# Two gate blocks in four by seven products, the retention norm on POOL and ScalarE, and gates that end with their chunks

## The chip, the core and the metric

One Trainium2 chip, one NeuronCore of it. TensorE (PE) multiplies, VectorE (DVE), ScalarE (ACT) and GpSimd (POOL) do the elementwise work, SyncE (SP) issues most of the transfers. Matrix products are accumulated in PSUM, eight banks of 128 x 512 float32. The metric is the device time of one execution in microseconds; lower is better. The kernel before takes 2174.5 us, the median of three runs (2174.4 to 2176.41).

## What is computed

A decoder block on 1024 tokens of width 1024 in float32: normalization and modulation, two token mixers side by side (chunkwise retention and dilated window attention), a gated merge, and an MLP. The change touches the retention mixer, four heads with key width 256 and value width 512, in chunks of 128 tokens:

```python
def step(state, inp):
    qi, ki, vi = inp
    s = jnp.einsum('bhid,bhjd->bhij', qi, ki) * inner_decay[None]
    o = (jnp.einsum('bhij,bhje->bhie', s, vi)
         + jnp.einsum('bhid,bhde->bhie', qi, state) * q_decay[None, :, :, None])
    state = (state * chunk_decay[None, :, None, None]
             + jnp.einsum('bhjd,bhje->bhde', ki * k_decay[None, :, :, None], vi))
    return state, o
...
ro = retention(rq, rk, heads(rv, RET_HEADS))
mu = jnp.mean(ro, axis=-1, keepdims=True)
var = jnp.mean(jnp.square(ro - mu), axis=-1, keepdims=True)
ro = ((ro - mu) * lax.rsqrt(var + GN_EPS)).transpose(0, 2, 1, 3).reshape(B, S, RET_V_W)
ro = (ro * gn_g.astype(jnp.float32) + gn_b.astype(jnp.float32)).astype(h.dtype)
ret_out = (jax.nn.silu(rg) * ro) @ w_ret_out
```

`rg` is a projection of the same normalized input to 2048 columns: 16 gate blocks of 128 columns, four for each head.

## The kernel before

Every float32 product is made of three products of rounded halves: a number is split into a high part (a copy on ACT) and a low part (a subtraction on DVE), and low x high, high x low and high x high are summed in PSUM (`mm3`, L207, L209, L211). One such product has 128 x 128 weights and 512 columns.

The stages follow one another, each written out in the order in which its engines are to work; every engine runs its own instructions in that order and waits where its inputs or a buffer are not ready. First values, then `queries_keys`, then `values`, then 32 steps `chunk(h, c)` (head h, chunk c), then attention, merge and MLP.

`queries_keys` runs a list of pairs (`PAIRS`). A pair is two blocks of 128 output columns against all 1024 inputs and tokens, done by a scheme that replaces eight block products by seven (`Blocks`, the seven in `ORDER`): 7 x 4 x 3 = 84 products in place of 2 x 48 = 96, for some additions and subtractions of weights and results on DVE. Queries, keys, attention queries, most branch gates and one Silu gate block of each head (`s_pairs`, two pairs) are made so and written to DRAM. After each product of a pair from item 116 on, and after each group of twelve products in `values`, `mod_turn` may issue an adaLN weight load on SP and reduce the one before on DVE.

A chunk (`chunk`) issues, on TensorE: the two halves of the new key-value product (`kv`), gate steps, scores and key transposes of the next chunk (`s_kt`), the output (`o`, from the carried state and from the scores), the four transposes of the chunk before's normalized output (`on_T`), and a last gate step. A gate step (`rg_mm`) is one of the eight k-slices of a gate block, six products; three blocks of each head are made in the chunks, 24 steps a head (`RG`), and a block's weights are split a step ahead by `ahead`. On the other engines: the state update on DVE (L743, L745) and its split on ACT and DVE (L749, L750); the split of the weights (L197, L198); the scores' decay and split and the keys' (L652 to L668); the queries' split on ACT and POOL (L616, L617); the statistics of the output and its normalization (L772 to L778), with POOL's power in between. In the first four chunks of a head, `u_final` finishes a quarter of the head before: two affine passes on ACT (L688), the multiplication with the Silu gate on DVE (L690), a store (L691).

PSUM in this stage: two double banks for gate blocks, and four single ones for everything else in a chunk, handed out as they come free. SBUF: a ring of twelve buffers of 128 x 1024 (`etile`) for transposed outputs and Silu gates.

Of the kernel before, what the change touches and what calls it, by code (L numbers as in the profile page):

```python
# [17 lines left out]
P = 128  # L18
# [22 lines left out]
CS_QD = 132  # L41
CS_QD2 = 136
# [98 lines left out]
def block_kernel(ctx, tc, io, stop=None, dbg=None):  # L141
# [12 lines left out]
    def banks(single):  # L154
# [7 lines left out]
        PS["n"] = 8 if single else 4  # L162
# [3 lines left out]
    def ps_mm(name):  # L166
        return PS["p"].tile([P, 2, 512], F32, tag="mm", bufs=2, name=name)

# [343 lines left out]
    def etile(name, dt=F32):  # L512
        return R["p"].tile([P, 1024], dt, tag="E", bufs=12, name=name)
# [116 lines left out]
    def s_kt(i):  # L630
# [34 lines left out]
        if pk is not None:  # L665
            nc.vector.scalar_tensor_tensor(flat(kl), flat(pk), kd, fv(flat(kh)), op0=ALU.mult, op1=ALU.subtract)
            hd["k", g] = (kh, kl)
        nc.vector.tensor_sub(sml, sm, fv(smh))  # L668

    def on_T(h, c):  # L670
# [3 lines left out]
        if c == 0:  # L674
            hd["on", h] = [etile(f"on{h}{e}") for e in range(4)]
        for e in range(4):
            nc.tensor.transpose(po[:, e, :], on[:, e * P:(e + 1) * P], ident)
        for e in range(4):
            nc.scalar.copy(hd["on", h][e][:, c * C:(c + 1) * C], po[:, e, :])

    def u_final(h, es=range(4), queue=nc.sync):
        for e in es:
# [7 lines left out]
            nc.vector.tensor_mul(t, t, hd["srg", h, e])  # L690
            queue.dma_start(y_d[h][:, 2 * (i % 2):2 * (i % 2) + 2, e // 2], t.rearrange("p (t x) -> p t x", t=2))  # L691

    RG = ((6, 2, 2, 3, 3, 3, 3, 2),) + ((3,) * NC,) * (H - 1)

    def rg_mm(n):

        for _ in range(n):
            if hd.get("rgk", NK) == NK:
                hd["rgk"], hd["rgw"], hd["rgp"] = 0, hd["rgws"].pop(0), ps_mm("rg")
            proj_mm(hd["rgp"], hd["rgw"], [hd["rgk"]])  # L700
            hd["rgk"] += 1
            if hd["rgk"] == NK:
                hd["rgs"] = hd["rgp"]

    def rg_out(h, c):

        if "rgs" in hd:
            e = {1: 0, 2: 0, 4: 1, 5: 1, 7: 2}[c]
            hd["srg", h, e] = etile(f"srg{h}{e}")
            nc.scalar.activation(hd["srg", h, e], flat(hd.pop("rgs")), AF.Silu)  # L710
        if c == 6:
            hd["srg", h, 3] = etile(f"srg{h}3")
            nc.sync.dma_start(hd["srg", h, 3], srg_d[h])

    def chunk(h, c, ahead, w=None):
# [21 lines left out]
        rg_mm(1 if g == 0 else RG[h][c] - 1)  # L737
# [9 lines left out]
        if g > 0:  # L747
            for i in range(len(kvs)):
                nc.scalar.copy(sh1[:, i, :], st[:, i, :])  # L749
                nc.vector.tensor_sub(sl1[:, i, :], st[:, i, :], fv(sh1[:, i, :]))  # L750
        if g == 0:
            jit_qk(2)
        ahead(2)
        if 0 < g < NG - 1:
            s_kt(g + 1)
# [12 lines left out]
        rg_mm(0 if g == 0 else 1)  # L768
        bn = p.tile([P, 6], F32, tag="bn", bufs=2, name=f"bn{h}{c}")
        ba = p.tile([P, 2], F32, tag="ba", bufs=2, name=f"ba{h}{c}")  # L770
        gr = p.tile([P, 1], F32, tag="gr", bufs=2, name=f"gr{h}{c}")
# [2145 lines left out]
```

## Time and profile before

| what | value |
|---|---|
| runs | 2174.4, 2174.5, 2176.41 us |
| profiled execution, its own time | 2173.28 us |
| its span, first to last instruction | 2171.3 us |
| pairs | about 180 to 598 us |
| values | about 598 to 712 us |
| retention chunks | about 712 to 980 us |
| bytes moved by transfers | 425.18 MB, 196 GB/s in the mean |
| granted TensorE clock | 0.999 |

Read such a profile by stages. A busy share says how much an engine worked, not whether it was waited for; a gap on TensorE in one stage has its own cause, which the lists of waits name. A matrix product is shown with its whole duration, from its first to its last column through the array, while the next one starts before it ends: the rate is seen in the distance of the starts.

### The profile page before, as it was taken

Reading aid. Unit: us, or ns where it says so; the run is one execution under the profiler, and the core shown is the slowest. Engines: PE = TensorE matmul, PEld = TensorE weight load, DVE = VectorE, ACT = ScalarE, POOL = GpSimd, SP = SyncE. Lnnn points to the kernel's source line nnn. Section 1 sums busy time; section 2 is a strip of 40 time slices with the busy share of each in tenths; the row PEclk is TensorE's granted clock in tenths of the full one; section 3 lists DMA queues with packets and bytes.
Section 4 is the critical chain, followed back from the end, with each engine's and each line's share of the span. In section 5 each row is a group of like instructions: output and inputs, shape, how many; then the busy total and the mean of one; then the engine's idle time right before and its main releaser. Section 6 shows DMA issues by size and latency. Waiting matters only on the chain. (4 is left out here: it accounts for less than half of the span.)

```text
span 2171.3 us, 27289 instructions
## 1 busy us (share of the span) xinstructions
PE 2144.7 (99%) x10036; PEld 1782.4 (82%) x10036; DVE 1520.4 (70%) x2358; ACT 959.3 (44%) x1757; POOL 165.7 (8%) x199
## 2 busy tenths in 40 slices
PE   8999999999999999999999999999999999999998
PEld 6888888888887788888888888888778888888887
DVE  6886777777656677776667644677876665877855
ACT  5543322323334455556656625434454455533413
POOL 0001111100001112211110000001000000000003
PEclk9999999999999999999999999999999999999999
DMA  9859998835588744436877366653144435645322
GB/s 383 282 208 309 285 306 265 243 117 194 186 301 303 234 148 151 160 127 197 218 194 196 115 245 211 217 191 132 64 175 160 150 136 193 253 135 173 109 88 78
DMA packets 162674, 425.18 MB, mean 196 GB/s; under 512 B 28005, under 2 KB 55916, under 8 KB 159468
## 3 DMA queue, kind: packets, MB, share of 16 engines
q1 hardware_dynamic: 150264, 374.90, 48.3%
q0 software_dynamic: 9584, 48.24, 9.9%
q8 instruction: 79, 1.29, 0.2%
q10 hardware_dynamic: 2692, 0.30, 0.1%
q14 instruction: 55, 0.45, 0.1%
HBM read 324.13 MB, written 160.32 MB: 223 GB/s over the span
## 5 line engine op out<-in xcount | busy, mean ns | idle before, releaser
L207 PE MATMUL qap<-hh,qaw 128*128 128x512 f32 x264 | 102.7, 389 | 0.0
L209 PE MATMUL qap<-hl,qaw 128*128 128x512 f32 x264 | 102.7, 389 | 0.0
L211 PE MATMUL qap<-hh,qaw 128*128 128x512 f32 x264 | 102.7, 389 | 0.0
L617 POOL TENSOR_TENSOR j<-qk,j 128x512 fp32r<-128x512 f32 x32 | 42.8, 1338 | 454.8 <-ACT j L616 454.8
L2235 POOL TENSOR_TENSOR accnf<-accnf,sqnf 128x256 f32<-128x256 f32 (+1 forms) x18 | 16.6, 922 | 609.6 <-ACT sqnf L2231 609.6
L2339 ACT ACTIVATE a<-a 128x512 f32<-128x512 f32 x48 | 30.3, 631 | 72.8 <-DVE a L2338 71.3
L749 ACT CAST stateh<-state 128x512 fp32r<-128x512 f32 x54 | 32.9, 622 | 57.8 <-DVE state L745 55.7
L209 PEld LDWEIGHTS qap<-hl,qaw 128*128 128x128 f32 x264 | 49.5, 188 | 10.4
L211 PEld LDWEIGHTS qap<-hh,qaw 128*128 128x128 f32 x264 | 49.6, 188 | 10.3
L207 PEld LDWEIGHTS qap<-hh,qaw 128*128 128x128 f32 x264 | 49.5, 188 | 10.2
L2547 ACT CAST w2h<-w2s 128x512 fp32r<-128x512 f32 x36 | 22.4, 621 | 80.3 <-DVE w2s L2585 80.3
L264 DVE TENSOR_TENSOR fw<-w1r,fw 128x512 fp32r<-128x512 f32 x48 | 32.9, 688 | 33.6 <-ACT fw L254 33.6
L264 DVE TENSOR_TENSOR qaw<-wa,qaw 128x512 fp32r<-128x512 f32 x66 | 44.0, 687 | 9.4 <-ACT qaw L254 9.4
L2070 DVE TENSOR_TENSOR rwl<-rwl,rwh 128x1024 fp32r<-128x1024 f32 x25 | 30.2, 1221 | 29.0 <-ACT rwh L2100 29.0
L207 PE MATMUL fp<-h2h,fw 128*128 128x512 f32 x128 | 50.0, 390 | 0.0
L209 PE MATMUL fp<-h2l,fw 128*128 128x512 f32 x128 | 49.8, 389 | 0.0
L211 PE MATMUL fp<-h2h,fw 128*128 128x512 f32 x128 | 49.8, 389 | 0.0
L207 PE MATMUL roa<-rh,rwl 128*128 128x512 f32 x128 | 49.8, 389 | 0.0
L209 PE MATMUL roa<-rl,rwh 128*128 128x512 f32 x128 | 49.8, 389 | 0.0
L211 PE MATMUL roa<-rh,rwh 128*128 128x512 f32 x128 | 49.8, 389 | 0.0
L1603 ACT ACTIVATE P<-P,ng 128x128 f32<-128x128 f32 (+1 forms) x96 | 41.9, 438 | 17.6 <-DVE ng L1595 17.5
L292 DVE TENSOR_TENSOR qat<-qat,qap 128x512 f32<-128x512 f32 x22 | 15.1, 688 | 42.8 <-PE qap L211 35.8
(3089 smaller groups left out, 7187.8 us busy)
## 6 DMA issues: line engine op xcount, KB each, us to landing
cossin<-in_w_ada_dram SPq DMA_DIRECT2D x32, 512.0 KB, 3.5
v<-vd SPq DMA_DIRECT2D x32, 512.0 KB, 4.3
w1r<-in_w_ff_dram SPq DMA_DIRECT2D x32, 512.0 KB, 4.6
yt<-y POOLq DMA_DIRECT2D x24, 512.0 KB, 7.5
xsd<-as SPq DMA_DIRECT2D x24, 512.0 KB, 3.1
w2r<-in_w_ff2s_dram SPq DMA_DIRECT2D x24, 512.0 KB, 6.4
em<-in_w_ada_dram SPq DMA_DIRECT2D x16, 512.0 KB, 10.2
wrvs<-in_w_rv_dram POOLq DMA_DIRECT2D x16, 512.0 KB, 9.8
```

The source lines that it names most:

```text
L207: nc.tensor.matmul(o, wl, xh, start=first, stop=False, skip_group_check=skip)
L209: nc.tensor.matmul(o, wh, xl, start=False, stop=False, skip_group_check=skip)
L211: nc.tensor.matmul(o, wh, xh, start=False, stop=last, skip_group_check=skip)
L264: nc.vector.tensor_sub(t[:, 512:], src, fv(t[:, :512]))
L292: nc.vector.tensor_sub(u, u, b)
L617: nc.gpsimd.tensor_sub(t[:, 1], src, fv(t[:, 0]))
L749: nc.scalar.copy(sh1[:, i, :], st[:, i, :])
L1603: nc.scalar.activation(v, v, AF.Exp, bias=ng[:, blk:blk + 1], accum_out=st[:, g, blk, 2 + a:3 + a])
L2070: nc.vector.tensor_sub(lo, fv(lo), fv(hi))
L2235: (nc.vector if f == 7 else nc.gpsimd).tensor_add(G["acc", key], G["acc", key], sq)
L2339: nc.scalar.activation(o, o, AF.Relu)
L2547: nc.scalar.copy(hi, src)
```

## The change

Two gate blocks of each head instead of one go through the pairs (four more blocks, two more pairs; each head now loads two from DRAM, in chunks 4 and 6), so that the chunks make two blocks, 16 steps a head, spread by `RG` so that a block ends with the last step of a chunk; the Silu follows at once. In PSUM a gate block takes two of three single banks, and five serve the rest; attention opens its own layout again. The ring for Silu gates has four buffers; transposed outputs have their own four, twice as wide, and are copied by two instead of four instructions.

The normalization is rewritten as scale x o + bias on ACT. The variance gets an epsilon that holds the decay, so no decay factor is left; POOL computes minus the mean, the power, and their product. Statistics now come on DVE before the second half of the state's low part, before the weights' split (`ahead`) and before the multiplication with the Silu gate, which is put off to the next chunk; the first half of the state's low part moves into the score chain (`mid`). `mod_turn` takes a step every second turn.

```diff
-    def banks(single):
+    def banks(single, ret=False):
 
         if PS:
             PS["ctx"].close()
@@ -159,12 +159,15 @@
         PS["ctx"] = ExitStack()
         PS["p"] = PS["ctx"].enter_context(tc.tile_pool(name=f"psum{PS['i']}", bufs=2, space=bass.MemoryType.PSUM,
                                                        reuse_waits="tile"))
-        PS["n"] = 8 if single else 4
+        PS["n"] = 8 if single else 5 if ret else 4
...
+    def ps_rg(name):
+        return PS["p"].tile([P, 512], F32, tag="rg", bufs=3, name=name)
...
-        return R["p"].tile([P, 1024], dt, tag="E", bufs=12, name=name)
+        return R["p"].tile([P, 1024], dt, tag="E", bufs=4, name=name)
...
-    def s_kt(i):
+    def s_kt(i, mid=None):
...
+        if mid:
+            mid()
         nc.vector.tensor_sub(sml, sm, fv(smh))
...
         if c == 0:
-            hd["on", h] = [etile(f"on{h}{e}") for e in range(4)]
+            hd["on2", h] = [R["p"].tile([P, 2, 1024], F32, tag="EO", bufs=4, name=f"on{h}{e}") for e in range(2)]
+            hd["on", h] = [hd["on2", h][e // 2][:, e % 2] for e in range(4)]
         for e in range(4):
             nc.tensor.transpose(po[:, e, :], on[:, e * P:(e + 1) * P], ident)
-        for e in range(4):
-            nc.scalar.copy(hd["on", h][e][:, c * C:(c + 1) * C], po[:, e, :])
-
-    def u_final(h, es=range(4), queue=nc.sync):
+        for e in range(2):
+            nc.scalar.copy(hd["on2", h][e][:, :, c * C:(c + 1) * C], po[:, 2 * e:2 * e + 2, :])
+
+    def u_final(h, es=range(4), queue=nc.sync, late=False):
         for e in es:
             i = h * 4 + e
             t = hd["on", h][e]
@@ -687,30 +693,36 @@
                 b = t[:, 512 * hf:512 * hf + 512]
                 nc.scalar.activation(b, b, AF.Identity, scale=gnv[0][:, neg + i:neg + i + 1],
                                      bias=gnv[1][:, neg + i:neg + i + 1])
-            nc.vector.tensor_mul(t, t, hd["srg", h, e])
-            queue.dma_start(y_d[h][:, 2 * (i % 2):2 * (i % 2) + 2, e // 2], t.rearrange("p (t x) -> p t x", t=2))
-
-    RG = ((6, 2, 2, 3, 3, 3, 3, 2),) + ((3,) * NC,) * (H - 1)
+
+            def mul(t=t, i=i, e=e):
+                nc.vector.tensor_mul(t, t, hd["srg", h, e])
+                queue.dma_start(y_d[h][:, 2 * (i % 2):2 * (i % 2) + 2, e // 2], t.rearrange("p (t x) -> p t x", t=2))
+
+            if late:
+                return mul
+            mul()
+
+    RG = (6, 2, 2, 2, 1, 1, 2, 3), (3, 2, 2, 2, 1, 1, 2, 3), (3, 2, 2, 2, 1, 1, 2, 3), (3, 2, 2, 2, 1, 1, 1, 1)
 
     def rg_mm(n):
 
         for _ in range(n):
             if hd.get("rgk", NK) == NK:
-                hd["rgk"], hd["rgw"], hd["rgp"] = 0, hd["rgws"].pop(0), ps_mm("rg")
+                hd["rgk"], hd["rgw"], hd["rgp"] = 0, hd["rgws"].pop(0), [ps_rg(f"rg{i}") for i in range(2)]
             proj_mm(hd["rgp"], hd["rgw"], [hd["rgk"]])
             hd["rgk"] += 1
             if hd["rgk"] == NK:
-                hd["rgs"] = hd["rgp"]
+                i = hd["rgi"] = hd.get("rgi", -1) + 1
+                t = hd["srg", i // 2, i % 2] = etile(f"srg{i // 2}{i % 2}")
+                for j, ps in enumerate(hd["rgp"]):
+                    nc.scalar.activation(t[:, 512 * j:512 * j + 512], ps, AF.Silu)
 
     def rg_out(h, c):
 
-        if "rgs" in hd:
-            e = {1: 0, 2: 0, 4: 1, 5: 1, 7: 2}[c]
+        if c in (4, 6):
+            e = c // 2
             hd["srg", h, e] = etile(f"srg{h}{e}")
-            nc.scalar.activation(hd["srg", h, e], flat(hd.pop("rgs")), AF.Silu)
-        if c == 6:
-            hd["srg", h, 3] = etile(f"srg{h}3")
-            nc.sync.dma_start(hd["srg", h, 3], srg_d[h])
+            nc.sync.dma_start(hd["srg", h, e], srg_d[h, e - 2])
 
...
-        rg_mm(1 if g == 0 else RG[h][c] - 1)
+        rg_mm(1 if g == 0 else RG[h][c] - (g < NG - 1))
         for i, kv in enumerate(kvs):
             if g == 0:
                 nc.scalar.copy(sh1[:, i, :], kv)
@@ -744,15 +756,17 @@
             else:
                 nc.vector.scalar_tensor_tensor(st[:, i, :], st[:, i, :], float(GAMMA[h] ** C), kv,
                                                op0=ALU.mult, op1=ALU.add)
-        if g > 0:
-            for i in range(len(kvs)):
+        def low(i):
+            nc.vector.tensor_sub(sl1[:, i, :], st[:, i, :], fv(sh1[:, i, :]))
+
+        if g > 0 and kvs:
+            for i in range(2):
                 nc.scalar.copy(sh1[:, i, :], st[:, i, :])
-                nc.vector.tensor_sub(sl1[:, i, :], st[:, i, :], fv(sh1[:, i, :]))
         if g == 0:
             jit_qk(2)
-        ahead(2)
+            ahead(2)
         if 0 < g < NG - 1:
-            s_kt(g + 1)
+            s_kt(g + 1, (lambda: low(0)) if kvs else None)
         po = ps_s(f"o{h}{c}")
         if c > 0:
             t = hd["j", g]
@@ -765,21 +779,28 @@
             jit_qk(g + 2)
         if g > 0:
             on_T(*divmod(g - 1, NC))
-        rg_mm(0 if g == 0 else 1)
+        rg_mm(1 if 0 < g < NG - 1 else 0)
         bn = p.tile([P, 6], F32, tag="bn", bufs=2, name=f"bn{h}{c}")
         ba = p.tile([P, 2], F32, tag="ba", bufs=2, name=f"ba{h}{c}")
-        gr = p.tile([P, 1], F32, tag="gr", bufs=2, name=f"gr{h}{c}")
+        gr = p.tile([P, 3], F32, tag="gr", bufs=2, name=f"gr{h}{c}")
         nc.vector.bn_stats(bn, po)
         nc.vector.bn_aggr(ba, bn)
-        nc.vector.tensor_scalar(gr, ba[:, 1:2], ct[:, CS_QD2 + h:CS_QD2 + h + 1], GN_EPS, op0=ALU.mult, op1=ALU.add)
-        nc.gpsimd.tensor_tensor(gr, gr, mhalf[:, 0:1], op=ALU.pow)
-        nc.vector.tensor_mul(gr, gr, ct[:, CS_QD + h:CS_QD + h + 1])
+        nc.vector.tensor_scalar_add(gr[:, 0:1], ba[:, 1:2], ct[:, CS_EQ + h:CS_EQ + h + 1])
+        nc.gpsimd.tensor_tensor(gr[:, 2:3], ba[:, 0:1], ct[:, CS_NEG:CS_NEG + 1], op=ALU.mult)
+        nc.gpsimd.tensor_tensor(gr[:, 1:2], gr[:, 0:1], mhalf[:, 0:1], op=ALU.pow)
+        nc.gpsimd.tensor_tensor(gr[:, 2:3], gr[:, 1:2], gr[:, 2:3], op=ALU.mult)
+        if g > 0:
+            if kvs:
+                low(1)
+            ahead(2)
+        if "um" in hd:
+            hd.pop("um")()
+        if h > 0 and c < 4:
+            hd["um"] = u_final(h - 1, (c,), late=True)
         on = p.tile([P, DV], F32, tag="on", bufs=1, name=f"onm{h}{c}")
-        nc.vector.tensor_scalar(on, po, ba[:, 0:1], gr, op0=ALU.subtract, op1=ALU.mult)
+        nc.scalar.activation(on, po, AF.Identity, scale=gr[:, 1:2], bias=gr[:, 2:3])
         hd["o", h, c] = on
         rg_out(h, c)
-        if h > 0 and c < 4:
-            u_final(h - 1, (c,))
 
...
-    srg_d = [dram.tile([P, S], F32, name=f"srgd{h}") for h in range(H)]
+    srg_d = {(h, i): dram.tile([P, S], F32, name=f"srgd{h}{i}") for h in range(H) for i in range(2)}
...
-    s_pairs = [("s", i) for i in range(H // 2)]
+    s_pairs = [("s", i) for i in range(H)]
     PAIRS = [{"r": r_pairs, "a": a_pairs, "g": g_pairs, "k": k_pairs, "s": s_pairs}[i].pop(0)
-             for i in "rargrarkrargrarkgagass"]
+             for i in "rargrarkrargrarkgagassss"]
...
             elif pair[0] == "s":
-                dst = srg_d[2 * pair[1] + i]
+                dst = srg_d[pair[1], i]
...
-        while turn["i"] < NV + 2 and 7 * turn["n"] > 16 * turn["i"]:
+        while turn["i"] < NV + 2 and turn["n"] > 2 * turn["i"]:
...
-        banks(False)
+        banks(False, True)
...
+    RGW, n = [], 0
+    for g in range(NG):
+        RGW += [g - (g > 2)] * (n < 8 * len(RGW) + 1 <= n + RG[g // NC][g % NC])
+        n += RG[g // NC][g % NC]
     for h in range(H):
         for c in range(NC):
             steps.add((lambda h, c: lambda ahead, *w: chunk(h, c, ahead, *w))(h, c),
-                      ([wsplit(io["w_rg"][3 * h + (0, 2, 5).index(c)])] if c in (0, 2, 5) else []),
+                      ([wsplit(io["w_rg"][RGW.index(NC * h + c)])] if NC * h + c in RGW else []),
                       manual=True)
...
+            if pair == a == 0:
+                banks(False)
...
-        cst[:, CS_QD + h] = np.exp(lg * (i + 1))
-        cst[:, CS_QD2 + h] = np.exp(2 * lg * (i + 1))
+        cst[:, CS_NEG] = -1.0
+        cst[:, CS_EQ + h] = GN_EPS * np.exp(-2 * lg * (i + 1))
...
-        "w_rg": _cols(w[:, 4096:6144].reshape(1024, 4, 4, P)[:, :, :3].reshape(1024, 1536)),
-        "w_rg2": _pairs(w[:, 4096:6144].reshape(1024, 4, 4, P)[:, :, 3].reshape(1024, 512)),
+        "w_rg": _cols(w[:, 4096:6144].reshape(1024, 4, 4, P)[:, :, :2].reshape(1024, 1024)),
+        "w_rg2": _pairs(w[:, 4096:6144].reshape(1024, 4, 4, P)[:, :, 2:].reshape(1024, 1024)),
```

4 lines of the change are left out of this document (2 added, 2 removed).

## The prediction

> **What bounds the kernel now.** I read the page first, then the busy times by stage, then the waits.
>
> ```profile
> span 2171.3 us, 27289 instructions
> ...
> PE 2144.7 (99%) x10036; PEld 1782.4 (82%) x10036; DVE 1520.4 (70%) x2358; ACT 959.3 (44%) x1757; POOL 165.7 (8%) x199
> ```
>
> ```profile
> 180.00:596.00 416.00, 416.00 (x1837) 344.47 (x1836) 303.74 (x472) 122.67 (x214) 36.33 (x50) 1.00 0.74 233
> 596.00:712.00 116.00, 112.84 (x493) 91.73 (x491) 71.34 (x99) 48.01 (x71) 8.33 (x10) 1.00 0.84 308
> ...
> 783.00:850.00 67.00, 66.94 (x334) 55.83 (x333) 51.25 (x108) 36.83 (x92) 14.40 (x16) 1.00 0.48 161
> ```
>
> Columns: stretch, length, busy time of PE, weight loads, DVE, ACT, POOL, granted clock, DMA share, GB/s. TensorE has no gap in the stage of pairs (180 to 596) and none in a head of retention chunks (783 to 850); only the value stage between them (596 to 712) shows 3.2 us of gap. So TensorE sets the time, by its number of products. In the pair stage 1837 products take 416.00 us, 0.2265 us each (one lasts longer, but they overlap). In a head DVE is busy 51 of 67 us, ACT 37: covered, as long as TensorE has filler between the steps of a chunk. The filler is the gate products, and the change takes a third of it away. One chunk of head 1, TensorE's timeline:
>
> ```profile
> 806.62 0.39 PE L207 MATMUL kv<-v,kl 128*128 128x512 f32 x1
> ...
> 810.71 0.28 PE L638 MATMUL sT<-j 128*128 128x256 f32 x1
> ...
> 811.27 0.48 PE L207 MATMUL o<-stateh,j 128*128 128x512 f32 x1
> ...
> 813.44 0.60 PE L677 MATMUL oT<-ct,onm 128*128 128x128 f32 x4
> ...
> 815.27 0.39 PE L207 MATMUL kv<-v,kl 128*128 128x512 f32 x1
> ```
>
> From kv to sT 4.09 us (kv's six products 1.37, two gate steps of six 2.72), scores and key transposes 0.56, output 2.17, output transposes and the last gate step 1.83; together 8.65. With n gate steps instead of three a chunk is 8.65 - 1.36 x (3 - n): 7.29 for two, 5.93 for one.
>
> **The change part by part.**
>
> *Products.* Four gate blocks leave the chunks (4 x 48 = 192 products) and come back as two pairs of 84 (168): 24 fewer, 24 x 0.2265 = -5.4 us. The pairs' adds lie under TensorE as those of the 22 pairs there do (DVE 304 of 416 us, no gap). The Trainium skill (TensorE: Matmul & The Clock Gate, Back-to-back issue gap) has streams of weight load and product of 512 columns come down to about 131 ns each, which would make this an estimate of -3.1, and it gives 216 ns only for a product by itself. The row's 226.5 ns, in a stage without a gap, decides.
>
> *Value stage.* The adaLN loads get a step every second turn instead of every 2.29. Before, the last step falls in turn 76 of 78; after, in turn 67 of 92, a turn being 12 products or 2.72 us: 68 us before the stage ends.
>
> ```profile
> SPq L1254 <- DVE cossin L1252: 36.7, 12, 9.0
> ```
> ```profile
> PE vc L209 <- DVE vwl L1328: 1.9, 2, 1.5
> ```
>
> SP's queue stood 36.7 us around this stage behind these loads, with the value weights behind it; TensorE waited 1.9 us for such weights about 20 turns into the value stage. After, that is turn 72, past the last step. Bounds 0 and -3.1 (all the stage's gap); I take -1.0, half the wait.
>
> *Work per chunk.*
>
> ```profile
> L750 DVE TENSOR_TENSOR statel<-state,stateh 128x512 fp32r<-128x512 f32 x28 | 18.1, 689 | 1.3
> L745 DVE SCALAR_TENSOR_TENSOR state<-state,kv 128x512 f32<-128x512 f32 x24 | 15.3, 680 | 0.0
> L778 DVE TENSOR_SCALAR onm<-o,ba,gr 128x512 f32<-128x512 f32 x17 | 13.8, 810 | 1.8
> L772 DVE BATCH_NORM_STATS2 bn<-o 128x6 f32<-128x512 f32 x16 | 11.1, 695 | 3.6 <-PE o L211 3.6
> L690 DVE TENSOR_TENSOR on<-on,srg 128x1024 f32<-128x1024 f32 x8 | 9.7, 1218 | 0.1
> L666 DVE SCALAR_TENSOR_TENSOR kl<-kT,ct,kh 128x256 fp32r<-128x256 f32 x14 | 6.7, 478 | 0.0
> L668 DVE TENSOR_TENSOR sml<-sm,smh 128x128 fp32r<-128x128 f32 x16 | 4.7, 293 | 0.7 <-ACT smh L664 0.7
> L654 DVE TENSOR_TENSOR sm<-sm,decay 128x128 f32<-128x128 f32 x16 | 4.7, 292 | 0.5
> L653 DVE TENSOR_TENSOR sm<-sm,sT 128x128 f32<-128x128 f32 x16 | 4.5, 284 | 7.0 <-ACT sm L652 7.0
> ...
> L774 DVE TENSOR_SCALAR gr<-ba,ct 128x1 f32<-128x1 f32 x16 | 3.4, 214 | 0.6
> L773 DVE BATCH_NORM_AGGREGATE ba<-bn 128x2 f32<-128x6 f32 x16 | 2.9, 183 | 0.5
> L776 DVE TENSOR_TENSOR gr<-gr,ct 128x1 f32<-128x1 f32 x16 | 2.6, 160 | 14.4 <-POOL gr L775 14.4
> ...
> L198 DVE TENSOR_TENSOR raw_6675l<-raw,raw_6675h 128x1024 fp32r<-128x1024 f32 x1 | 1.2, 1227 | 0.3 <-ACT raw_6675h L197 0.3
> ```
> ```profile
> L749 ACT CAST stateh<-state 128x512 fp32r<-128x512 f32 x29 | 17.7, 622 | 30.5 <-DVE state L745 28.4 <-DVE state L743 2.0
> L688 ACT ACTIVATE on<-on,gnt 128x512 f32<-128x512 f32 x16 | 12.4, 837 | 0.0
> ...
> L710 ACT ACTIVATE srg<-rg 128x1024 f32<-128x1024 f32 x7 | 7.4, 1050 | 1.9 <-PE rg L211 1.9
> L663 ACT ACTIVATE kh<-kT,ct 128x256 fp32r<-128x256 f32 x14 | 6.7, 478 | 0.0
> ...
> L652 ACT COPY sm<-sT 128x128 f32<-128x128 f32 x16 | 4.2, 263 | 12.3 <-PE sT L640 12.2
> ...
> L197 ACT CAST raw_6675h<-raw 128x1024 fp32r<-128x1024 f32 x1 | 1.0, 1045 | 0.0
> ```
> ```profile
> L617 POOL TENSOR_TENSOR j<-qk,j 128x512 fp32r<-128x512 f32 x16 | 20.7, 1294 | 103.4 <-ACT j L616 103.4
> L775 POOL TENSOR_TENSOR gr<-gr,ct 128x1 f32<-128x1 f32 x16 | 8.7, 544 | 0.9 <-DVE gr L774 0.9
> ```
> ```profile
> L763 ACT COPY state<-kv x2: 578/584/590, 725.3 to 725.7; 128x512 f32<-128x512 f32 x2
> ```
>
> The numbers after the bar are the group's busy time, the mean of one in ns and the idle time ahead of it. DVE loses the normalization (0.81), the product with the decay (0.16) and its wait for POOL (0.9): off the path today, so worth nothing by themselves. The normalization on ACT has two pointer operands and reads PSUM: between 0.58 (L763) and 0.84 (L688); I take 0.80, for its operands are L688's. By the Trainium skill (ScalarE: Activation LUTs, What ACT_TABLE_LOAD costs) each pointer operand adds about 93 ns: an estimate of 0.58 + 0.19 = 0.77, which moves the sum by less than 0.1 us a chunk. POOL's two new products are 0.3 to 0.54 each (its row for the power, or less); 0.45 taken. A head's DVE work falls from 51 to about 45 us in 67 - 11 = 56: not the bound on average. What remains is order, in four places.
>
> (a) *The split of the second gate block's weights, chunk 2 of head 0.* It moves from ahead of the scores to the end of chunk 1, on ACT behind the Silu that ends there. With K the start of chunk 2's kv: last gate product lands at K + 0.16, Silu in two halves to K + 1.26 (1.05 to 1.17; 1.1 taken), high copy 1.05 to K + 2.3, DVE's low part 1.22 to K + 3.5. TensorE wants it at K + 1.37, behind kv. +2.1 us (1.9 to 2.8, the upper if DVE is late). Before, the same split ran ahead of the score chain.
>
> (b) *Gate bank after chunk 6.* Three single banks hold one and a half blocks; the next block's second product (0.23 us on) needs the bank that the first Silu half reads. Chunk 7 has no kv between: 0.16 + 0.03 + 0.58 - 0.23 = 0.54 us in three heads, +1.6 (0 if the Silu half is hidden; 3.2 if it is both halves).
>
> (c) *The Silu of chunk 1, heads 1 to 3.* Four buffers hold the Silu gates, all four still full of the head before; the first is freed by its multiplication, which now comes in this very chunk, on DVE behind statistics (0.69 + 0.18 + 0.21) and low part (0.69), itself 1.22: 2.99 after the output, which ends at K - 1.66. The Silu starts at K + 1.36, its first half ends at K + 1.95; the next block's second product is due at K + 1.60. 0.35 us, and about as much again where DVE comes to the statistics late: +0.65 x 3 = 2.0 (0 to 3.0). Behind the waiting Silu on ACT stand two affine passes (1.55 together), the normalization, and the state copies of chunk 2.
>
> (d) *One-step chunks.* In chunk 4 DVE has 2 x 0.68 + 0.28 + 0.29 + 0.48 + 0.69 + 0.29 + 1.09 + 0.69 + 1.22 = 6.4 us against TensorE's 5.93, and its score chain waits for ACT's state copies. In order, from chunk 4's kv: DVE ends chunk 3's multiplication at 1.3 (as in (c), 2.99 after an output that ended 1.66 before), state updates to 2.0 and 2.7, ACT's state copies to 2.6 and 3.3, score copy 3.6, key copy 4.0, DVE's key low part 4.6, state's first low part 5.3, scores' low part 5.6, statistics (their output landed at 4.3, so they are 1.3 late) to 6.7, second low part 7.4, multiplication 8.6. Steps that follow without a wait overlap a little, so some 0.5 comes off: 8.1, which is 2.1 into chunk 5. Chunk 5's first kv bank is then read at about 2.8, and chunk 4's normalization (statistics 6.4, power 0.54, product 0.45, ACT 0.80) frees its bank at 8.3, 2.3 in. Chunk 5's output wants a bank at 1.37 + 0.56 = 1.93, and of the five small banks two hold its kv, two its scores and keys, one chunk 4's output: 0.4 to 0.9, 0.6 taken, in heads 1 to 3, +1.8 (0 to 2.7). Heads without such multiplications, and the last head's other one-step chunks, have DVE at 5.2 and go free.
>
> *Priced at nothing.* The two wider output copies in place of four (0.28 each) lie on ACT behind the transposes, with TensorE in a gate step; without that cover they would save 0.1 a chunk. Statistics ahead of the second low part: the low part is read by the next chunk's output, over 4 us on. The gate multiplication a chunk later delays a store that attention reads only after the last chunk. The two gate loads per head go out on SP at chunks 4 and 6, behind fetches for three chunks on, into buffers freed by then; uncovered, SP would hold the next fetch by the landing, but three chunks are 18 us. POOL's queue: the three small operations follow the 1.29 us subtraction, as the power does today. SP's gate loads find free buffers.
>
> Sum: -5.4 - 1.0 + 2.1 + 1.6 + 2.0 + 1.8 = +1.1 us. Profiled: 2173.28, span 2171.3 and 2.0 around it; 1.2 below the runs' median. 2174.5 + 1.1 = **2175.6**.
>
> **The rivals.**
> *Faster, 2168.* The four waits are covered as every chain is today, and the value stage gets its 1.9 us: 2174.5 - 5.4 - 1.9 = 2167.2, one microsecond left over. For it: no gap in 67 us now, DVE and ACT with less work. Against: (a) is a straight sum.
> *Slower, 2181.* One mechanism: ACT's queue in chunk 1 of heads 1 to 3. Silu to K + 2.4, affine passes to 4.0, normalization to 4.8, state copies to 6.0, score and key copies to 6.7, DVE's key low part 7.2; chunk 3's kv wants it at K + 7.3. From 0.1 us of further lateness TensorE waits, and chunks 2 to 5 inherit it: about 1.8 us a head, 5.4 in all, 2181. For it: nothing in the queue can pass the held Silu. Against: TensorE's own waits in (c) move the due time too.
> *The fresh bank layout*: the first key tile of attention falls on the bank of chunk 31's output, freed some 3 us after it: +2.6, 2178.
>
> **How the numbers follow.** A measurement tells 0.2% from no change, 4.3 us. Forecast 0.38; bank layout 0.05, which lies within 0.2% too: 0.43 together. Faster rival 0.25, slower rival 0.32, each beyond 0.2%; the bounds of (a) to (d) together reach +11.7 - 5.4, another 6.3 above, so it is the heavier side. Range 2167 (faster case) to 2184 (slower case with (a) at its upper bound).
>
> **What would show it.** Right: 24 pairs at 19.0 us each; the chunk stage, 712 to 980 us now, 268 less 43.5 plus 7.5, about 232; TensorE waiting for the gate weights' low part once by about 2 us, for Silu halves in heads' chunks 2 and 7, for banks in chunks 4 to 5; the value stage with under 2.5 us of gap. Wrong: chunk gaps under 2 us in all (faster), gaps of over 1 us in chunk 3 or 4 of each head (slower), or gaps in the pairs.

## The result and the profile after

The changed kernel takes 2187.88 us (median of 5 runs, 2186.16 to 2189.86), the kernel before 2174.5: a ratio of 1.0061, 95% interval 1.0049 to 1.0072. It is slower, by 13.4 us where 1.1 were forecast, and above the range's end of 2184. The profiled execution took 2189.86 us against 2173.28 before. Its page begins:

```profile
span 2188.1 us, 27357 instructions
...
PE 2146.4 (98%) x10012; PEld 1782.1 (81%) x10012; DVE 1504.3 (69%) x2322; ACT 981.8 (45%) x1749; POOL 207.1 (9%) x263
```

TensorE has 24 products fewer, and still a longer span. By stages (columns as in the prediction: stretch, length, busy PE, weight loads, DVE, ACT, POOL, granted clock, DMA share, GB/s):

```profile
180.00:636.00 456.00, 456.00 (x2013) 377.75 (x2012) 335.27 (x524) 136.76 (x238) 36.22 (x50) 1.00 0.75 233
636.00:748.00 112.00, 110.91 (x488) 91.09 (x488) 61.28 (x79) 48.25 (x71) 7.13 (x10) 1.00 0.77 282
748.00:996.00 248.00, 228.87 (x1128) 186.98 (x1127) 161.18 (x353) 150.94 (x324) 97.88 (x126) 0.99 0.51 166
```

The pairs are without a gap, now 24 of them, and the value stage's gap has gone from 3.2 to 1.1 us. The chunk stage is what went wrong: it took 268 us, should have lost 43.5 of them and taken on 7.5, and takes 248, with 19 us of gap. TensorE's waits in that stage (what waits, for what, us in all, times, longest):

```profile
PE o L210 <- ACT onm L801: 10.5, 12, 1.3
PE rg L210 <- ACT srg L718: 3.8, 6, 1.3
PE ak L210 <- DVE raw_7244l L201: 2.9, 1, 2.9
PE rg L210 <- DVE raw_5632l L201: 1.8, 1, 1.8
```

More than half is one wait: the output `o` cannot start until ScalarE has normalized the chunk before's output. The timeline of one-step chunks 4 and 5 of head 1 shows why (start, duration, engine, line, operation, and in brackets the idle time ahead of it and what ended it):

```profile
847.34 0.78 ACT L801 ACTIVATE onm<-o,gr 128x512 f32<-128x512 f32 x1 [1.77 <-POOL gr L791]
...
848.02 1.13 ACT L764 CAST stateh<-state 128x512 fp32r<-128x512 f32 x2
...
848.17 0.51 PE L210 MATMUL o<-stateh,j 128*128 128x512 f32 x1 [1.28 <-ACT onm L801]
...
849.05 0.27 ACT L655 COPY sm<-sT 128x128 f32<-128x128 f32 x1
...
849.35 0.29 DVE L656 TENSOR_TENSOR sm<-sm,sT 128x128 f32<-128x128 f32 x1 [1.52 <-ACT sm L655]
...
851.07 0.69 DVE L786 BATCH_NORM_STATS2 bn<-o 128x6 f32<-128x512 f32 x1
...
852.27 0.75 POOL L789 TENSOR_TENSOR gr<-ba,ct 128x1 f32<-128x1 f32 x1
852.29 0.68 DVE L760 TENSOR_TENSOR statel<-state,stateh 128x512 fp32r<-128x512 f32 x1
...
852.89 1.22 DVE L698 TENSOR_TENSOR on<-on,srg 128x1024 f32<-128x1024 f32 x1
852.98 1.53 POOL L790 TENSOR_TENSOR gr<-gr,ct 128x1 f32<-128x1 f32 x1
...
854.02 1.28 DVE L757 SCALAR_TENSOR_TENSOR state<-state,kv 128x512 f32<-128x512 f32 x2
...
854.59 0.19 POOL L791 TENSOR_TENSOR gr<-gr 128x1 f32<-128x1 f32 x1
...
854.82 0.78 ACT L801 ACTIVATE onm<-o,gr 128x512 f32<-128x512 f32 x1 [3.19 <-POOL gr L791]
...
855.65 0.50 PE L210 MATMUL o<-stateh,j 128*128 128x512 f32 x1 [1.29 <-ACT onm L801]
```

This is a closed loop. Normalization at 847.34; behind it on ScalarE, in order, the state copies and the score copy; VectorE's score chain can start at 849.35 (2.01 later) and reaches the statistics at 851.07 (+1.72); POOL starts at 852.27 (+1.20); the next normalization is at 854.82 (+2.55). Sum 7.48 us, and no gate step is in it. VectorE's own round is nearly as long: behind the statistics it has a low part, the gate multiplication and the state updates, which end at 855.30, 0.19 us before ScalarE's next state copies start. TensorE's own work in a one-step chunk is 5.93 us, so it waits, for a bank as is tested below, in chunk 4 and again in chunk 5. In the kernel before a chunk has 8.65 us of TensorE work, and its list of waits has none of the output on the normalization.

What VectorE runs beside POOL's power belongs to the length. Head 0 has no head before it, and so no multiplication (L698). There two normalizations start at 786.62 and 793.10, 6.48 us apart, with a power of 0.54 us between them. The next starts 7.47 us later, at 800.57: the low part of new weights (L201, 1.22 us) stands where the multiplication stands above, and the power takes 1.53.

### The profile page after: what moved, and what is told of

Its sections match the earlier page's. It is cut to its first block, busy times and chain, and to the rows that moved or that the text cites. A ratio compares the mean times of both kernels' runs of the same rounds, so it can differ in the third digit from the quotient of the medians.

```text
span 2188.1 us, 27357 instructions
## 1 busy us (share of the span) xinstructions
PE 2146.4 (98%) x10012; PEld 1782.1 (81%) x10012; DVE 1504.3 (69%) x2322; ACT 981.8 (45%) x1749; POOL 207.1 (9%) x263
## 3 DMA queue, kind: packets, MB, share of 16 engines
q8 instruction: 79, 1.29, 0.2%
## 5 line engine op out<-in xcount | busy, mean ns | idle before, releaser
L210 PE MATMUL qap<-hh,qaw 128*128 128x512 f32 x288 | 112.1, 389 | 0.0
L212 PE MATMUL qap<-hl,qaw 128*128 128x512 f32 x288 | 112.1, 389 | 0.0
L214 PE MATMUL qap<-hh,qaw 128*128 128x512 f32 x288 | 112.1, 389 | 0.0
L2262 POOL TENSOR_TENSOR accnf<-accnf,sqnf 128x256 f32<-128x256 f32 (+1 forms) x18 | 16.6, 922 | 609.6 <-ACT sqnf L2258 609.6
L214 PEld LDWEIGHTS qap<-hh,qaw 128*128 128x128 f32 x288 | 54.1, 188 | 11.2
L212 PEld LDWEIGHTS qap<-hl,qaw 128*128 128x128 f32 x288 | 54.1, 188 | 11.2
L210 PEld LDWEIGHTS qap<-hh,qaw 128*128 128x128 f32 x288 | 54.1, 188 | 11.2
L267 DVE TENSOR_TENSOR qaw<-wa,qaw 128x512 fp32r<-128x512 f32 x72 | 48.1, 686 | 10.9 <-ACT qaw L257 10.9
L656 DVE TENSOR_TENSOR sm<-sm,sT 128x128 f32<-128x128 f32 x32 | 9.2, 288 | 64.1 <-ACT sm L655 64.1
L801 ACT ACTIVATE onm<-o,gr 128x512 f32<-128x512 f32 x32 | 24.9, 777 | 46.9 <-POOL gr L791 46.8
```

The lines of the kernel that those rows point to most:

```text
L210: nc.tensor.matmul(o, wl, xh, start=first, stop=False, skip_group_check=skip)
L212: nc.tensor.matmul(o, wh, xl, start=False, stop=False, skip_group_check=skip)
L214: nc.tensor.matmul(o, wh, xh, start=False, stop=last, skip_group_check=skip)
L267: nc.vector.tensor_sub(t[:, 512:], src, fv(t[:, :512]))
L656: nc.vector.tensor_add(sm, sm, ps[:, C:2 * C])
L801: nc.scalar.activation(on, po, AF.Identity, scale=gr[:, 1:2], bias=gr[:, 2:3])
```

## Experiments

Distances from one chunk's first `kv` product to the next one's, head 1, from the timelines, in us; the second column says how many gate steps lie in the first six chunks. They carry most of what follows. The names e6, e9 and so on are those of the runs below.

| kernel | gate steps | c0 | c1 | c2 | c3 | c4 | c5 |
|---|---|---|---|---|---|---|---|
| before | 3 3 3 3 3 3 | 7.24 | 8.64 | 8.96 | 8.65 | 8.65 | 8.64 |
| changed | 3 2 2 2 1 1 | 7.24 | 8.10 | 8.87 | 7.61 | 7.47 | 7.49 |
| e6, gates only | 3 2 2 2 1 1 | 7.24 | 7.29 | 8.00 | 8.06 | 8.08 | 8.40 |
| e9, even | 2 2 2 2 2 2 | 5.89 | 7.35 | 7.30 | 7.92 | 7.30 | 7.64 |
| e6e, gates only, even | 2 2 2 2 2 2 | 5.89 | 7.29 | 9.27 | 8.07 | 8.15 | 7.46 |
| e12, power alone, at once | 3 2 2 2 1 1 | 7.24 | 7.60 | 8.08 | 7.33 | 7.60 | 7.57 |

### The change in two halves

The first theory was that POOL's three operations, held up by what VectorE does beside them, with ScalarE's normalization behind them and the late weight splits, make the loss. Gates only (e6):

```diff
-        nc.gpsimd.tensor_tensor(gr[:, 2:3], ba[:, 0:1], ct[:, CS_NEG:CS_NEG + 1], op=ALU.mult)
         nc.gpsimd.tensor_tensor(gr[:, 1:2], gr[:, 0:1], mhalf[:, 0:1], op=ALU.pow)
-        nc.gpsimd.tensor_tensor(gr[:, 2:3], gr[:, 1:2], gr[:, 2:3], op=ALU.mult)
+        nc.vector.tensor_mul(gr[:, 1:2], gr[:, 1:2], ct[:, CS_ONE:CS_ONE + 1])
...
-        nc.scalar.activation(on, po, AF.Identity, scale=gr[:, 1:2], bias=gr[:, 2:3])
+        nc.vector.tensor_scalar(on, po, ba[:, 0:1], gr[:, 1:2], op0=ALU.subtract, op1=ALU.mult)
```

> The two gate blocks of seven products, the RG table, the banks and the Silu straight into SBUF stay; the normalization (VectorE, with POOL's power between two VectorE operations), the low parts, the weight splits and the scaling of the head before go back to their old places. Theory (the loss is POOL's three small operations, slowed by what VectorE does beside them, ScalarE's normalization behind them, and the late weight splits): the output's waits for a bank that the normalization frees fall from 10.5 to under 3 us, the 2.9 and 1.8 us waits for the splits vanish, and the time is 2168 to 2173. Rival (one-step chunks are too short for five small banks, whoever normalizes): the output's waits stay at 7 us or more and the time is over 2179.

Measured 2189.18 us (ratio 1.0067, 1.0052 to 1.0082): as slow as the whole change. TensorE's waits in the chunk stage:

```profile
PE kv L210 <- DVE kl L669: 7.5, 13, 0.8
PE o L210 <- DVE onm L793: 5.6, 9, 0.7
PE rg L210 <- ACT srg L718: 2.4, 3, 0.8
```

The splits came in time but for 0.5 us at attention, and POOL's hold-up was gone (its power took 0.544 us in the mean), but VectorE, now with the normalization again, came late with the keys' low part and the banks. Chunks 2 to 5 take 8.0 to 8.4 us with two steps or one. The theory failed in this form; the rival had the time right but not the wait, which was under 7 us at the bank and 7.5 elsewhere.

Normalization only (e7), in the kernel before (the lines above the other way round, with the new places of low parts, weights and gate multiplication):

```diff
-        nc.vector.tensor_scalar(on, po, ba[:, 0:1], gr, op0=ALU.subtract, op1=ALU.mult)
+        nc.scalar.activation(on, po, AF.Identity, scale=gr[:, 1:2], bias=gr[:, 2:3])
```

> Only the normalization by POOL and ScalarE, its statistics ahead of the low part and the weights, and the late gate multiplication are put into the kernel before; three gate blocks, three products to a chunk and four small banks stay. Theory: the new chain behind the output costs time by itself, less than in the changed kernel since each chunk has more products to cover it: the first attention weights come 2.5 to 3 us late with some 1.6 us of low clock, and the output waits 2 to 6 us for banks: 2178 to 2184. Rival (the loss comes from the gate products taken out of the chunks): 2174.5 or less, no wait of the output on the normalization over 0.3 us.

Measured 2177.07 us (ratio 1.0011, 1.0002 to 1.0021), below what the theory gave and above what the rival gave. The one new wait of size is attention's first weights:

```profile
PE ak L207 <- DVE raw_7735l L198: 1.7, 1, 1.7
```

The list has no wait of the output on the normalization. So the new chain is nearly free where each chunk has three steps, and both halves lose when steps are taken away: the loss seems to belong to chunks that have become shorter than the work that goes round behind their outputs. The next run tests it.

### Is it the chunk's length? Even products

The same 64 steps, spread evenly (e9):

```diff
-    RG = (6, 2, 2, 2, 1, 1, 2, 3), (3, 2, 2, 2, 1, 1, 2, 3), (3, 2, 2, 2, 1, 1, 2, 3), (3, 2, 2, 2, 1, 1, 1, 1)
+    RG = ((6, 2, 2, 2, 1, 1, 1, 1),) + ((2,) * NC,) * (H - 1)
```

> The changed kernel with the gate products spread evenly: 6, 2, 2, 2, 1, 1, 1, 1 steps in the chunks of head 0 and 2 in every chunk of the other heads (64 steps as before, each gate block still ends with a chunk). Theory (a chunk needs some 7.5 us for the chain statistics, POOL, ScalarE, bank; a chunk with one step gives TensorE 5.9 us of work and one with two 7.3): in heads 1 to 3 the output's waits fall from 10.2 to 2 to 4 us, the Silu waits from 3.8 to under 1, the late splits stay: 2178 to 2181. Rival (over a head VectorE, ScalarE and POOL have a fixed amount to do behind which TensorE waits, however the products lie): the waits move to other chunks and the time stays at 2186 to 2189.

Measured 2174.49 us (ratio 1.0002, 0.9992 to 1.0011): the whole loss against before is gone, more than the theory gave, with one line. Waits in the chunk stage, and POOL's power there (32 times, busy us and mean ns behind the bar):

```profile
PE ak L210 <- DVE raw_7390l L201: 2.9, 1, 2.9
PE rg L210 <- DVE raw_5632l L201: 1.8, 1, 1.8
PE o L210 <- ACT onm L801: 1.3, 4, 0.4
```
```profile
L790 POOL TENSOR_TENSOR gr<-gr,ct 128x1 f32<-128x1 f32 x32 | 29.0, 908 | 1.0 <-DVE gr L788 0.7
```

The output's waits fell from 10.5 to 1.3 us and the Silu waits vanished, though the power still takes 908 ns: with 7.3 us of TensorE work in a chunk the loop of 7.5 is covered but for tenths. The loop itself is still there: three normalizations of head 1 start at 834.05, 841.52 and 848.99 us, 7.47 apart each time. The next one, with no multiplication beside POOL's power (0.54 us), comes after 6.47, and there the engines catch up. The fixed-amount rival fell.

### Is it the bank?

Six small banks (e8):

```diff
-        return PS["p"].tile([P, 512], F32, tag="rg", bufs=3, name=name)
+        return PS["p"].tile([P, 512], F32, tag="rg", bufs=2, name=name)
...
-        PS["n"] = 8 if single else 5 if ret else 4
+        PS["n"] = 8 if single else 6 if ret else 4
```

> The changed kernel with six small PSUM banks and two gate banks instead of five and three. Theory (the output waits for a bank, and the late normalization only holds it): the output's waits on the normalization fall from 10.5 to under 2 us, and the gate block's start waits for both Silu halves instead, 0.5 to 1.3 us at each of seven: 2182 to 2188. Rival (the output waits for data, not for a bank): its waits stay at 9 us or more and the Silu waits come on top: 2191 to 2195.

Measured 2188.59 us (two runs), just beyond the theory's range. No wait of the output on the normalization is left in the list; in its place:

```profile
PE rg L210 <- ACT srg L718: 9.9, 6, 2.3
```

Chunk 4 now runs at 5.93, as the prediction had it without waits, and chunk 5 at 6.30. So the output waits for a bank and not for data. The loop is hidden here and not shorter: the normalizations of chunks 3 and 4 still start 7.47 us apart (838.92 and 846.39). The sixth bank is paid by the gate block, whose start now waits longer for the Silu, and in chunk 2 the Silu itself stands 3.19 us for the late multiplication (828.28, behind L698). A second payment is not in the list of waits: chunk 2 of heads 1 to 3 takes 11.2 to 11.7 us, some 2 us more than 7.29 and its wait, and the granted clock in these chunks is 0.85.

### Is it POOL?

POOL's power has a mean of 1032 ns in the changed kernel against 544 before, and 1.53 us beside VectorE's 1.22 us multiplication in the timeline above. First, POOL keeps the power alone (e2):

```diff
-        nc.gpsimd.tensor_tensor(gr[:, 2:3], ba[:, 0:1], ct[:, CS_NEG:CS_NEG + 1], op=ALU.mult)
         nc.gpsimd.tensor_tensor(gr[:, 1:2], gr[:, 0:1], mhalf[:, 0:1], op=ALU.pow)
-        nc.gpsimd.tensor_tensor(gr[:, 2:3], gr[:, 1:2], gr[:, 2:3], op=ALU.mult)
+        nc.vector.tensor_scalar(gr[:, 2:3], ba[:, 0:1], gr[:, 1:2], -1.0, op0=ALU.mult, op1=ALU.mult)
```

> The changed kernel with POOL keeping the power alone; the product of mean and 1/deviation is one VectorE operation right behind it, so VectorE stands still while POOL works. Theory (POOL's operations are held up by VectorE's two-operand work beside them): POOL's power falls from a mean of 1.14 us to 0.55 in every chunk, the output's waits for the normalization fall from 10.5 us to 2 to 4, and the time to 2180 to 2183. Rival 1 (POOL's operations are slow for another reason, such as the subtraction ahead of them): power still 0.9 or more. Rival 2 (ScalarE's order, not POOL, sets the normalization): power is short and the output's waits stay at 8 us or more, 2186 to 2189.

Measured 2193.72 us (ratio 1.009, 1.0073 to 1.0106): slower still. The power went to 544 ns and the output's waits to 4.0 us, as expected, but the late multiplication came later on a VectorE that stands still, and the Silu waited for its buffer:

```profile
PE rg L210 <- ACT srg L718: 11.6, 6, 2.9
...
PE o L210 <- ACT onm L800: 4.0, 5, 0.8
```

Second, the changed kernel with VectorE's later work ahead of the statistics (e3; the same lines are taken out behind POOL's operations):

```diff
+        if g > 0:
+            if kvs:
+                low(1)
+            ahead(2)
+        if "um" in hd:
+            hd.pop("um")()
+        if h > 0 and c < 4:
+            hd["um"] = u_final(h - 1, (c,), late=True)
         nc.vector.bn_stats(bn, po)
```

> The changed kernel with the low part, the weights and the late gate multiplication ahead of the output's statistics instead of behind them, so that VectorE has nothing of two operands beside POOL's three operations. Theory (POOL's operations are held up by VectorE's two-operand work): POOL's power falls from a mean of 1.03 us to 0.55 to 0.6 in all chunks, the chain from statistics to normalization is shorter, but starts later, by the 0.7 to 2.6 us of the work moved ahead: 2186 to 2194. Rival (power is slow behind another POOL operation, whatever VectorE does): its mean stays at 0.9 or more.

Measured 2210.04 us (two runs), far beyond what was expected, with POOL's operations all short (the power, up to 996 us, and the new wait):

```profile
L796 POOL TENSOR_TENSOR gr<-gr,ct 128x1 f32<-128x1 f32 x29 | 15.8, 545 | 3.0
```
```profile
PE o L210 <- DVE state L757: 16.4, 11, 2.9
```

That POOL is held up by what VectorE runs beside it is shown; that it makes the loss is not. The Trainium skill (SBUF — State Buffer, Who interferes with whom, and the rules of its summary) has GpSimd and a VectorE operation with two SBUF inputs share a port pair that the one locks for its whole instruction; the 0.54 against 1.53 agree, though the second operand by itself was not varied here.

Third, the gate multiplication at once, not a chunk later, first alone (e4):

```diff
-            hd["um"] = u_final(h - 1, (c,), late=True)
+            u_final(h - 1, (c,))
```

> The changed kernel with the gate multiplication of the head before done at once, in the chunk of its scaling, and not a chunk later. Theory (the Silu of chunk 1 in heads 1 to 3 waits for a buffer that the late multiplication frees): the waits of about 1 us of the first gate product of chunk 2 (3.1 us in heads 1 to 3) vanish; the multiplication's wait for ScalarE holds VectorE up instead, so the output's waits grow: 2185 to 2190. Rival (those waits are for the PSUM banks alone): they stay.

Measured 2183.68 us (ratio 1.0034, 1.002 to 1.0049), better than expected:

```profile
PE o L210 <- ACT onm L801: 10.6, 13, 1.2
...
PE rg L210 <- ACT srg L718: 0.7, 3, 0.2
```

The Silu waits of chunk 2 were for the buffer, as the prediction's (c) had it; the output's waits kept their sum and moved, in head 1 from 0.57, 1.28 and 1.29 us in chunks 1, 4 and 5 to 1.08, 1.21, 0.86 and 0.29 in chunks 1, 3, 4 and 5. In the profiled executions about 1.5 us of the gain is a clock that did not fall (below). Then both edits together (e12):

> The changed kernel with both single edits together: POOL keeps the power alone, VectorE multiplies mean and 1/deviation right behind it, and the gate multiplication of the head before is done at once. Theory (POOL's held-up operations make up a good half of the output's waits; with them short these waits fell to 4.0 us, and only the Silu buffers, now freed at once, gave it back): output's waits 4 to 6 us against 10.6 with the multiplication at once alone, Silu waits under 2 us, 2177 to 2180. Rival (VectorE's standing still costs what POOL's shorter operations give, whatever frees the buffers): 2183 to 2187, with waits on VectorE's state or keys, or the Silu waits back at over 6 us.

Measured 2185.79 us (ratio 1.0047, 1.0031 to 1.0064): the rival's time. The output's waits are 6.1 us, but from head 1's first `kv` to head 2's it takes 60.5 us, with the multiplication at once alone 60.4. The loop goes another way now, in head 1:

```profile
844.63 0.78 ACT L800 ACTIVATE onm<-o,gr 128x512 f32<-128x512 f32 x1 [0.49 <-DVE gr L790]
...
845.05 1.22 DVE L698 TENSOR_TENSOR on<-on,srg 128x1024 f32<-128x1024 f32 x1
...
846.19 1.28 DVE L757 SCALAR_TENSOR_TENSOR state<-state,kv 128x512 f32<-128x512 f32 x2
...
846.90 1.22 ACT L764 CAST stateh<-state 128x512 fp32r<-128x512 f32 x2 [1.50 <-DVE state L757]
...
850.05 0.69 DVE L786 BATCH_NORM_STATS2 bn<-o 128x6 f32<-128x512 f32 x1
...
851.35 0.54 POOL L789 TENSOR_TENSOR gr<-gr,ct 128x1 f32<-128x1 f32 x1
...
852.23 0.78 ACT L800 ACTIVATE onm<-o,gr 128x512 f32<-128x512 f32 x1 [1.90 <-DVE gr L790]
```

ScalarE's state copies wait 1.50 us for VectorE, which stood for POOL and then had low part, multiplication and state to do: 844.63 to 852.23 is 7.60 us, against 7.48 with POOL held up. VectorE pays by its waiting what POOL gains. The single cause first suspected is thereby a link of the loop, worth nothing when it is shortened by letting VectorE stand still. Both ways round have the multiplication in them.

### The late weights

The weights' loads and splits ahead of the scores again (e1):

```diff
         if g == 0:
             jit_qk(2)
-            ahead(2)
+        ahead(2)
...
                 low(1)
-            ahead(2)
```

> The changed kernel with the next weights (their loads and their split) back ahead of the next chunk's scores in every chunk. Theory: the waits of 2.9 us (first attention key weights) and 1.8 us (second gate block) vanish, and with them the two stretches of low granted clock behind them (3.4 us): 2179 to 2181. Rival (the low clock has another cause and stays): 2182.5 to 2184. Other rival (the split's two operations only delay the statistics, so the output's waits grow by as much): 2186 to 2189.

Measured 2181.59 us (ratio 1.0035, 1.0022 to 1.0048). The 1.8 us wait of the second gate block is gone, attention's is shorter, not gone, and the granted clock is 1.00 from 985 to 1015 us:

```profile
PE o L210 <- ACT onm L800: 8.0, 9, 1.3
...
PE ak L210 <- DVE raw_7193l L201: 1.8, 1, 1.8
```

Both edits, early weights and even products (e10):

> The even products together with the weights' loads and splits back ahead of the scores. Theory: both gains add, waits of the chunk stage under 6 us in all: 2171 to 2175. Rival (the split ahead of the statistics takes from VectorE what the even chunks gave): 2177 to 2181.

Measured 2175.95 us (ratio 1.0012, 1.0002 to 1.0021), between the two forecasts and no better than even products alone: the late weights are gone, but

```profile
PE o L210 <- ACT onm L800: 5.1, 5, 1.6
PE sT L641 <- POOL j L620: 2.5, 1, 2.5
```

The output's waits of 1.3 to 1.6 us come in the chunk of each of heads 1 to 3 that has a split ahead of its statistics (its low part itself stood 1.7 to 2.3 us on VectorE for ScalarE's high copy): there it lengthens the loop. The wait for `j` has the same source, in chunk 6 of head 0: ScalarE's copy of the scores (L667) stands 1.65 us for VectorE, which has the split's low part (800.60, 1.22 us) ahead of the score chain, and the queries' copy, from which POOL makes `j`, stands behind it on ScalarE. So the weights go early only where they are late, in chunks 1 and 31, on top of the even products (e11):

```diff
+        if g in (0, 1, NG - 1):
+            ahead(2)
...
-            ahead(2)
+            if 1 < g < NG - 1:
+                ahead(2)
```

> The even products, and the weights' loads and splits ahead of the scores in chunks 1 and 31 alone, the two places whose splits come late. Theory (two waits of 1.8 and 2.9 us and the low clock behind them are all that is left of the loss, and elsewhere the split belongs behind the statistics): the chunk stage's waits fall from 6.8 to 2 to 3 us: 2167 to 2170. Rival (as with all splits early: what they take from the statistics is lost again at the bank): 2173 to 2176.

Measured 2169.56 us (7 runs, 2168.34 to 2170.39; ratio 0.9974, 0.9963 to 0.9985), faster than both kernels:

```profile
PE o L210 <- ACT onm L803: 1.2, 4, 0.5
PE ak L210 <- DVE raw_7390l L201: 0.7, 1, 0.7
...
PE kv L210 <- DVE kl L669: 0.6, 1, 0.6
```

### Is the new normalization needed, then?

The gates-only kernel with the even products (e6e):

> The gates-only kernel (normalization and order of before) with the even products. Theory (with the old normalization VectorE sets a chunk of 8.0 to 8.1 us in heads 1 to 3, whether it has one step or two, so spreading the steps cannot help it): chunks of heads 1 to 3 stay at 7.9 to 8.2 us and the time at 2184 to 2189; the new normalization is then worth some 10 to 14 us in the even table. Rival (short chunks alone are to blame, with either normalization): waits fall as in the changed kernel, 2173 to 2178.

Measured 2185.85 us (ratio 1.0047, 1.0033 to 1.006), the time that the theory gave:

```profile
PE kv L210 <- DVE kl L669: 8.2, 8, 1.9
PE sT L641 <- POOL j L620: 5.8, 3, 3.7
```

With the old normalization VectorE is busy 48.2 of 60 us (808 to 868 us), and chunks 1 to 5 of head 1 take 8.05 us in the mean, though from 7.3 to 9.3 and not 7.9 to 8.2 each; with the new one it is 43.8, and 7.50 in the mean. In the even table the new normalization and its order are worth some 10 us (ratios to the kernel before of 1.0047 and 1.0002). Part of this is the early split of this kernel: its wait of 3.7 us for `j` is the one just described, and against early weights with the new normalization (e10, 1.0012) it is some 8 us. The new normalization and its order are what lets the gate products leave.

## Why the prediction was wrong, point by point

- **Products, -5.4: right.** 2013 products in 456.00 us are again 0.2265 us each; 24 pairs of 19.0 us.
- **Value stage, -1.0: right in kind, small.** The gap fell by 2.1 us; the last adaLN step starts at 680.3 us, 68 us before the stage ends, as forecast (before, at 706.2 of 712), and the wait of 1.9 us for `vwl` is not in the list any more. Whether the earlier loads did it was not tried by itself.
- **(a) Split of the second gate block, +2.1: right.** 1.8 us, in chunk 2 of head 0.
- **(b) Gate bank after chunk 6, +1.6:** 0.22 us in three heads, 0.7 in all, inside its bounds.
- **(c) Silu of chunk 1, +2.0: right, but small.** 1.28, 0.93 and 0.91 us, 3.1 in all, just above its upper bound of 3.0; the multiplication at once removed them.
- **(d) One-step chunks, +1.8: the step that failed,** with 10.5 us. Of these, 3.9 lie in chunk 5 of heads 1 to 3, where the prediction had its 1.8, 3.6 in chunk 4, 2.8 in the two-step chunks 1 and 3, and 0.3 in head 0. The prediction saw the right bank and a right chunk, but followed the lag once, from chunk 4 into chunk 5, and let it end there. It is a loop: the normalization holds back ScalarE's state copies, these the score chain, that the statistics, these POOL, and POOL the next normalization. The even products show it: with 7.3 us of work in each chunk the same loop costs 1.3 us in all. With the multiplication beside POOL's power, the loop of 7.48 us sets every chunk with less TensorE work than that; with nothing beside it, in head 0, the loop is 6.48. POOL's part was taken as 0.54 + 0.45 and measures 0.75 + 1.53 + 0.19. With the forecast's values this way round would have come to 6.0, but VectorE's, only 0.19 us behind it, would then have held it up. So POOL's price alone would not have mended the term: with a short power and VectorE standing still the loop is 7.60.
- **Priced at nothing, and wrongly:** the weights' split behind the statistics in chunk 31, where attention's first key weights are made: 2.9 us. The prediction costed this move at the second gate block only.
- **Not in the sum: the clock.** Behind two of these waits it fell (last section). Chunk 2 of head 0 takes 10.9 us, and 9.4 in a kernel with the same wait and a full clock: 1.5. From attention's late weights to its score product that waits for `kl` it is 17.7 us, and 16.1 with the even products, where the clock did not fall: 1.6. Together 3.1.

Against the forecast that makes 8.7 (d) + 2.9 (chunk 31) + 3.1 (clock) + 1.1 (c) - 0.9 (b) - 0.3 (a) - 1.1 (values) = 13.5 us; the medians differ by 12.3, the profiled execution by 15.5 (16.6 - 1.1). The sum counts waits alone, and an interval grows by more than its wait: chunk 4 of head 1 is 1.54 us over its 5.93, of which 1.28 are the wait.

The range's upper end does not follow from its working: the slower case, 2181, with (a) at its upper bound, 0.7 more, is 2181.7 and not 2184. The rival at 2181 (ScalarE's queue in chunk 1, the keys' low part late for `kv`) does not show: `kv` waits for nothing. Its notion that later chunks inherit the lag was right, on another path. The fresh bank layout does not show either: attention's first product waits for VectorE's low part of the weights, and with these in time (e11) 0.7 us are left of it. The faster rival's premise, that chains are covered as today, holds once the products are spread and the two splits early: 2169.56 against its 2168.

## What to carry to other kernels

Before filler work is taken out of a loop, follow the chain that runs behind the loop's output around until it meets itself, over all engines with their orders and buffers; its length is a floor for the passes, and passes below it pay each time, not once. A spare buffer can hide the floor for a pass or two and does not lower it (e8). Spread the filler so that no pass falls far under that floor, since an average that fits says nothing. A step moved behind other work has to be priced at each place where its result is wanted, the first instruction of the next stage included.

## What was not expected of the hardware

The granted clock falls after some waits of 1.8 to 2.9 us, and not after others. Two stretches of the changed kernel, then the first in the kernel with the multiplication at once, then the stretch behind attention's 2.9 us wait in the kernel with even products:

```profile
762.00:782.00 20.00, 18.17 (x86) 15.02 (x86) 12.04 (x26) 12.23 (x26) 6.21 (x11) 0.91 0.41 126
...
990.00:1000.00 10.00, 7.06 (x27) 5.53 (x26) 3.54 (x5) 5.05 (x8) 1.29 (x5) 0.84 0.24 76
```
```profile
762.00:782.00 20.00, 18.17 (x93) 14.87 (x92) 13.26 (x30) 13.54 (x30) 6.30 (x9) 1.00 0.38 119
```
```profile
985.00:1000.00 15.00, 14.75 (x71) 12.07 (x70) 9.44 (x8) 10.05 (x14) 3.55 (x5) 1.00 0.53 185
```

In the last of these the wait ends at 981.58, and straight behind it, from 981.5 to 985, the clock is 1.00 too. The 1.8 us wait at about 770 us is in seven of these kernels; in four of them the clock is 0.91 in that stretch, in three 1.00, and the chunk takes 10.9 us in the former and 9.4 in the latter: 1.5 us that a single profile can't be asked to repeat. The Trainium skill (TensorE: Matmul & The Clock Gate, What's actually happening) has a free-running window of about 3.4 us and a clock that drops after at least one idle window. That it comes and goes agrees with a window that no kernel starts; that 1.8 us can do it differs, being half a window, and here the measurement decides.

POOL's 128 x 1 operations are priced by their neighbours: the product with minus one takes 0.75 us beside VectorE's low part in the timeline above, and 0.19 in the mean where nothing ran beside it (POOL undisturbed), the power 1.53 and 0.54.
